# Transposes in blocks, queries and keys in one product, and a reordered opening in a two-layer encoder trunk

## The chip, the cores and the metric

The kernel runs on one core of a Trainium2 chip. The metric is device time in microseconds (us) of the one launch; lower is better. The kernel before takes 2476.66 us, the median of 3 runs (2476.47 to 2478.3).

## What is computed

A float32 input x of 256 tokens by 2048 features goes through two layers. Each layer is a normalised mixer with a residual, then a normalised gated feed-forward part with a residual, and a final RMSNorm follows. The reference, cut to its frame:

```python
for layer in range(DEPTH):                      # DEPTH = 2
    y = rmsnorm(h, ln_mix[layer])
    if layer % 2 == 0:                          # A: 8 heads x 3 dilated groups; B: 4 differential heads
        mix = even_mixer(y, ev_w_in[e], ev_w_out[e], ..., t5_table, lambda_init)
    else:                                       # C: 8 grouped-query heads with rotary; D: 8 neighbourhood heads
        mix = odd_mixer(y, od_w_in[o], od_w_out[o], gqa_q_norm[o], gqa_k_norm[o], na_rpb[o], rows)
    h = h + mix
    f = conv_ffn(rmsnorm(h, ln_ffn[layer]), ffn_w_up[layer], ffn_conv_w[layer], ffn_conv_b[layer], ffn_w_down[layer])
    h = h + f
return rmsnorm(h, ln_final)
```

The weights are float32 and are read once: 459 MB in all, for only 256 tokens.

## The kernel before

**Products in two parts.** Each float32 operand is split into a high and a low part, so that three fast products (high by high, high by low, low by high) give nearly full precision. ScalarE writes the high part (`S.copy`, L214), VectorE the low part (L217). A piece of a weight matrix, a *unit*, is 128 x 1024 numbers: `wunit` (L106) loads it on SP's queue into one of 5 buffers `raw` and splits it into `wh` and `wl`, of which there are 4 each.

**Two kinds of product.** `gemm_a` (V, output and down projections) takes the activations as the stationary operand and has 512 output columns; a unit has 12 matmuls of 512 columns (L178 to L180). The other kind takes a weight tile as the stationary operand and has [high | low] activations of 256 tokens as the moving one. It consists of H, a matmul with `wh` of 512 columns (`b_high`, L126), and L, a matmul with `wl` of 256 columns (`b_low`, L132). An output tile of 128 features needs 2 units, 16 H and 16 L. `gemm_b` makes one tile in the order 8 H, 8 L, 8 L, 8 H. `gemm_b2`, used in the feed-forward part, makes two tiles: 32 H, then 32 L.

**The order of the work.** Program order is written by hand. A small planner holds attention work back: `later(delay, fn, rank)` puts a piece into a list, and every `tick()` in the products moves a counter on by one and emits what is due, values (rank 0) before transposes (rank 1) before logits and softmax (rank 2). A query tile and a key tile are two calls of `gemm_b` (in `qk_tile`), each with its own tick; the attention on them has a delay of 2. A scheduler then goes through the program in that order and issues, on each engine, the first instruction that its own model takes to be ready; so instructions can move past each other within an engine, unless `tc.keep_in_program_order` pins one behind its predecessor on that engine.

**Transposes.** The residual `h` is turned into feature-major tiles `yT` by TensorE transposes into PSUM (`transposes`, L260). Two buffers `tp`, of one bank each, take four transposes each; two of them make one `yT` tile, which ScalarE and VectorE then read out and split (`y_tile`). In the program two transposes are followed by the reading of their half of the bank, and then by the next two. `to_features` (L735) and `b_finish` (L636) do the same. Softmax maps are transposed four at a time (`transposed_probs`, L363).

**The opening.** Eight steps `u` each load two tiles of x and a unit for two V products (`v_ps`), and between them: the rows of x (`x_rows`), their squares for the norm (`squares`), the loads (`rel_loads`, on SP) and the making (`rel_tables`) of a table of position biases, which takes two matmuls with a onehot matrix (L430, L431), an add (L433) and stores on GpSimd's queue. `row_factor` and `row_broadcast` make the norm's factor per token.

Of the kernel before, what the change touches and what calls it, by code (L numbers as in the profile page):

```python
# [58 lines left out]
def trunk_kernel(ctx: ExitStack, tc, a, out):  # L59
# [61 lines left out]
    def two(ap):  # L121
        return ap.rearrange("p (a b) -> p a b", a=2)
# [11 lines left out]

    def gemm_b(src, act):

        ps = two(tps("gm", 4))
        wh, wl = wunit(src[0])
        b_high(ps, wh, 0, act)
        b_low(ps, wl, 0, act)  # L140
        wh, wl = wunit(src[1])
        b_low(ps, wl, 1, act)
        b_high(ps, wh, 1, act)
        tick()
        return ps

    def gemm_b2(srcs, act, middle=lambda: None):

        pss = [two(tps("gm", 4)) for _ in srcs]
        low = []  # L150
        for u in range(2):
            for ps, src in zip(pss, srcs):
                wh, wl = wunit(src[u])
                b_high(ps, wh, u, act, last=False)
                low.append((ps, wl, u))
            if u == 0:
                middle()
# [5 lines left out]
        tick()  # L163
        return pss
# [75 lines left out]

    def squares(c, ts=(0, 1)):
        if c == 0:
            ssq_now[0] = tmp.tile([P, 2, 4], F32, name=nm("ssq"), tag="ssq")
        for t in ts:
            junk = tmp.tile([P, 512], F32, name=nm("junk"), tag="junk", bufs=1)
            S.activation(junk, hchunk(t, c), AF.Square, accum_out=ssq_now[0][:, t, c:c + 1])

    def y_tile(src, gain, kt, pin=False):
        y = acts.tile([P, 2, SEQ], F32R, name=nm("yT"), tag="yT", bufs=KT)
        split_scaled(y[:, 0, :], y[:, 1, :], src, gain[:, kt:kt + 1], pin)  # L250
        return y

    def transposes(c, gain, res):

        for b in range(2):
            ps = two(tps("tp", 2))
            for j in range(2):
                kt = c * 4 + b * 2 + j
                for t in range(2):
                    T.transpose(ps[:, j, t * P:(t + 1) * P], h[:, t, kt * P:(kt + 1) * P], ident)  # L260
                res.append(y_tile(ps[:, j, :], gain, kt))

    def row_factor():
        ss = tmp.tile([P, 2], F32, name=nm("ss"), tag="ss")
        V.tensor_reduce(ss, ssq_now[0], axis=AX.X, op=ALU.add)
        return rsqrt_mean(ss, D, "rstd", const)

    def row_broadcast(rstd, by_parity=False):

        ps = tps("tp", 2)  # L270
        for t in range(2):
            b = tmp.tile([P, P], F32, name=nm("rb"), tag="rb")
            V.tensor_copy(b, rstd[:, t:t + 1].to_broadcast([P, P]))
            T.transpose(ps[:, t * P:(t + 1) * P], b, ident)
# [43 lines left out]

    def qk_tile(src, act, r, order, slot):
        t = halves(gemm_b(src, act), r, order)  # L320
        y = new_qk("qk", slot)
        split(y[:, 0, :], y[:, 1, :], t)
        return y

# [33 lines left out]
    def transposed_probs(p0, p1, order=None):  # L358

        ps = two(tps("tp", 2))  # L360
        for kt in range(2):
            for t, p in enumerate((p0, p1)):
                T.transpose(ps[:, kt, t * P:(t + 1) * P], p[:, kt * P:(kt + 1) * P], ident)  # L363
        pt = new_pt()
        split(pt[:, :, 0, :], pt[:, :, 1, :], order(ps) if order else ps)
        return pt
# [54 lines left out]

    def rel_tables():

        table, onehot, bmask, bmask2 = rel_in
# [5 lines left out]
        T.matmul(ps[0:28, :], th, oh, start=True, stop=False)  # L430
        T.matmul(ps[0:28, :], tl, oh, start=False, stop=True)  # L431
        vals = tmp.tile([28, NREL + 1], F32, name="vals", tag="rw", bufs=1)
        V.tensor_tensor(vals, ps[0:28, :], bmask, op=ALU.add)  # L433
        G.dma_start(rel, vals)
        vals2 = tmp.tile([28, 256], F32, name="vals2", tag="t0")
        V.tensor_tensor(vals2, ps[0:28, :].rearrange("p (j r) -> p r j", r=2)[:, 1, :], bmask2, op=ALU.add)
        G.dma_start(rel2, vals2)

    rstd_par = const.tile([P, 2], F32, name="rstd_par")

    def parity_factor(R):

        ps = two(tps("tp", 2))
        for t in range(2):
            T.transpose(ps[:, t, 0:P], R[:, t * P:(t + 1) * P], ident)
        V.tensor_copy(rstd_par, ps[:, :, 0])

    v_ps = [[tps("gm", 4), tps("gm", 4)] for _ in range(2)]
    for u in range(8):
        xt = att.tile([P, 2, SEQ], F32, name=nm("xT"), tag=f"qk{2 + u % 4}", bufs=1)  # L450
        nc.sync.dma_start(xt.rearrange("p a b -> p (a b)"), a["xT"][u])
        x_tile(xt, u, 0)
        if u:
            x_tile(xt, u, 1)
        for g in range(2):
            a_unit(v_ps[g], a["eva_v"][g], u, yT, KT, parts=1 if u else 2,
                   between=None if u or g else lambda: x_tile(xt, 0, 1))
# [12 lines left out]
        tick()  # L470
# [72 lines left out]
    def a_head(hd, vg):  # L543
        sc = []
        for g in range(3):
            b = a_bias(hd, g)
            q = qk_tile(a["eva_qk"][hd * 6 + 2 * g], yT, Rq, rev, 2 * g)
            k = qk_tile(a["eva_qk"][hd * 6 + 2 * g + 1], yT, R, None, 2 * g + 1)
            if g == 0:
                later(2, lambda q=q, k=k, b=b: a_local(q, k, b, sc))  # L550
            else:
                later(2, lambda g=g, q=q, k=k, b=b: a_strided(g, q, k, b, sc))

        def soft():
            softmax(sc[0])
            later(2, lambda: a_transposes(sc[0], hd, vg), 1)
        later(2, soft)

    for hh in range(2):
        vg = []  # L560
        for g in range(3):
            ps = v_ps.pop(0) if v_ps else gemm_a(a["eva_v"][hh * 3 + g], yT, KT)
            if hh and g == 0:
# [68 lines left out]
    def b_finish(hd, o):  # L632
        ps = two(tps("tp", 2))
        for f in range(2):
            for t in range(2):
                T.transpose(ps[:, f, t * P:(t + 1) * P], o[:, t, f * P:(f + 1) * P], ident)  # L636
            y = new_act("mix", 8 + 2 * hd + f)
# [3 lines left out]
    for pair in range(2):  # L641
        vt = v_tiles(gemm_a(a["evb_v"][pair], yT, KT), rstd_par, range(20 - 4 * pair, 24 - 4 * pair))
        for hd in (2 * pair, 2 * pair + 1):
            bias = row_bias(24 + hd)
            sc = []
            for m in range(2):
                q = qk_tile(a["evb_qk"][hd * 4 + m], yT, Rq, rev, 2 * m)
                k = qk_tile(a["evb_qk"][hd * 4 + 2 + m], yT, R, None, 2 * m + 1)
                later(2, lambda m=m, q=q, k=k, sc=sc, bias=bias: b_logits(m, q, k, sc, bias))
# [4 lines left out]
    def ffn(layer, yT, gain, last=False):  # L654
        R = None
        res = None
        for half in range(2):
            prod = []
            for i in range(HALF_F):
                f = half * HALF_F + i  # L660
                srcs = [a["up"][layer, f, x] for x in range(2)]
                if f == 0:
# [4 lines left out]

                    pg, pu = gemm_b2(srcs, yT, first_units)
                else:
                    pg, pu = gemm_b2(srcs, yT)  # L670
                g = halves(pg, R)
# [57 lines left out]
    def to_features(ys, nh, slot):  # L729
        res = []  # L730
        for i in range(nh):
            if i % 2 == 0:
                ps = two(tps("tp", 2))
            for t in range(2):
                T.transpose(ps[:, i % 2, t * P:(t + 1) * P], ys[t][:, i, :], ident)  # L735
            q = new_qk("cq", slot + i)
            split(q[:, 0, :], q[:, 1, :], ps[:, i % 2, :])
            res.append(q)
        return res
# [52 lines left out]
    for hh in range(2):  # L792
        vt = v_tiles(gemm_a(a["od_v"][hh], yT, KT), rstd, ((18, 19, 20, 21), (16, 17, 22, 23))[hh])
        for hd in range(hh * 4, hh * 4 + 4):
# [6 lines left out]
            G.tensor_tensor(y, y, colmask.unsqueeze(1).to_broadcast([P, 6, 64]), op=ALU.add)  # L801
            q = qk_tile(a["od_qk"][hd * 2], yT, Rq, rev, hd % 2 * 2)
            k = qk_tile(a["od_qk"][hd * 2 + 1], yT, R, None, hd % 2 * 2 + 1)
            later(2, lambda hd=hd, q=q, k=k, vt=vt, y=y: d_head(hd, q, k, vt, y))
# [181 lines left out]
```

## Time and profile before

| | |
|---|---|
| median of 3 runs | 2476.66 us (2476.47 to 2478.3) |
| profiled execution | 2478.31 us, span 2476.5 us |
| TensorE matmuls | busy 2465.1 us (100%), 13113 of them |
| TensorE weight loads | busy 2124.5 us (86%) |
| VectorE, ScalarE | busy 1624.0 us (66%), 1252.4 us (51%) |
| GpSimd | busy 43.9 us (2%) |
| moved by DMA | 463.60 MB, mean 187 GB/s |

A profile is one execution. In the rows of the timeline the first number is the start in us from the start of the span, the second the time covered; then come engine, line, operation, output<-input and the count, and in brackets the idle time before and what ended it. Matmuls are pipelined, so that the durations of neighbours overlap: what one costs is read from start to start.

### The profile page before, as it was taken

The numbers are of one execution on the slowest core, as the hardware profiler recorded it, in microseconds if no ns is written. First come the engines' busy times: TensorE is split into PE (matmuls) and PEld (weight loads), VectorE is DVE, ScalarE is ACT, GpSimd is POOL, SyncE is SP. The second block draws the span as 40 slices with busy tenths as digits, with TensorE's granted clock in tenths as the row PEclk, the third lists the DMA queues.
The fourth block names the chain that finished last, engine by engine and source line by source line (L and its number), as shares of the span: only waits on it lengthen the run. The fifth ranks groups of instructions, "written<-read, shape, count | busy, mean of one in ns | idle before, by whom it ended". The sixth has DMA issues, their size and how long they took to land.

```text
span 2476.5 us, 34420 instructions
## 1 busy us (share of the span) xinstructions
PE 2465.1 (100%) x13113; PEld 2124.5 (86%) x13113; DVE 1624.0 (66%) x2462; ACT 1252.4 (51%) x1862; POOL 43.9 (2%) x71
## 2 busy tenths in 40 slices
PE   9999999999999999999999999999999999999998
PEld 7888888888888888888888888888888888888887
DVE  6676567676576775467775568665677655676754
ACT  6455455465555453445444457545554533545443
POOL 0000000000000000000000000100000000000000
PEclk9999999999999999999999999999999999999999
DMA  8655566556555556656556555765565566555564
GB/s 296 188 175 178 186 180 184 176 177 181 173 178 185 197 181 207 192 176 199 183 198 193 187 186 164 174 177 179 172 200 182 194 199 194 185 186 189 194 198 144
DMA packets 130282, 463.60 MB, mean 187 GB/s; under 512 B 15248, under 2 KB 15788, under 8 KB 130116
## 3 DMA queue, kind: packets, MB, share of 16 engines
q1 hardware_dynamic: 127124, 455.03, 56.2%
q0 software_dynamic: 2560, 6.08, 2.7%
q8 instruction: 102, 1.67, 0.3%
q14 instruction: 64, 0.52, 0.1%
q10 hardware_dynamic: 432, 0.30, 0.0%
HBM read 459.16 MB, written 2.18 MB: 186 GB/s over the span
## 4 chain that ended last, share of the span: by engine, by line
PE 100%; DVE 0%; ACT 0%; issue 0%; DVEq 0%
PE gm L126 38%; PE gm L132 20%; PE gm L179 13%; PE gm L180 13%; PE gm L178 13%; PE tp L363 0%; PE tp L260 0%; PE s L340 0%; PE s L339 0%; PE s L341 0%; PE s L534 0%; PE s L503 0%; PE s L401 0%; PE s L375 0%; PE s L527 0%; PE s L374 0%
## 5 line engine op out<-in xcount | busy, mean ns | idle before, releaser
L217 DVE TENSOR_TENSOR wl<-raw,wh 128x1024 fp32r<-128x1024 f32 (+1 forms) x858 | 1039.0, 1221 | 557.6 <-ACT wh L214 389.8
L214 ACT CAST wh<-raw 128x1024 fp32r<-128x1024 f32 (+1 forms) x858 | 899.7, 1049 | 735.9 <-PE gm L180 419.4
L126 PE MATMUL gm<-yT,wh 128*128 128x512 f32 x4096 | 974.1, 391 | 0.0
L126 PEld LDWEIGHTS gm<-yT,wh 128*128 128x128 f32 x4096 | 754.5, 188 | 148.4 <-DVE yT L223 0.7
L132 PEld LDWEIGHTS gm<-yT,wl 128*128 128x128 f32 x4096 | 513.5, 191 | 13.3
L132 PE MATMUL gm<-yT,wl 128*128 128x256 f32 x4096 | 517.6, 283 | 0.0
L207 ACT COPY t<-gm 128x256 f32<-128x256 f32 x256 | 95.4, 373 | 360.3 <-PE gm L132 203.6
L178 PE MATMUL gm<-wh,prod 128*128 128x512 f32 x704 | 274.6, 390 | 0.0
L180 PE MATMUL gm<-wh,prod 128*128 128x512 f32 x704 | 274.2, 390 | 0.0
L179 PE MATMUL gm<-wl,prod 128*128 128x512 f32 x704 | 274.0, 389 | 0.0
L208 DVE TENSOR_TENSOR t<-t,gm 128x256 f32<-128x256 f32 x256 | 106.4, 416 | 101.2 <-ACT t L207 101.2
L179 PE MATMUL gm<-wl,yT 128*128 128x512 f32 x416 | 163.6, 393 | 1.6 <-DVE wl L217 1.6
L178 PE MATMUL gm<-wh,yT 128*128 128x512 f32 x416 | 163.4, 395 | 0.0
L180 PE MATMUL gm<-wh,yT 128*128 128x512 f32 x416 | 163.4, 393 | 0.0
L179 PEld LDWEIGHTS gm<-wl,prod 128*128 128x128 f32 x704 | 132.2, 188 | 27.3
L178 PEld LDWEIGHTS gm<-wh,prod 128*128 128x128 f32 x704 | 132.2, 188 | 27.2
L180 PEld LDWEIGHTS gm<-wh,prod 128*128 128x128 f32 x704 | 132.1, 188 | 27.2
L178 PE MATMUL gm<-wh,mix 128*128 128x512 f32 x256 | 101.1, 395 | 0.0
L179 PE MATMUL gm<-wl,mix 128*128 128x512 f32 x256 | 100.4, 392 | 0.0
L180 PE MATMUL gm<-wh,mix 128*128 128x512 f32 x256 | 100.3, 393 | 0.0
L179 PEld LDWEIGHTS gm<-wl,yT 128*128 128x128 f32 x416 | 79.1, 190 | 17.6 <-DVE wl L217 2.0
L180 PEld LDWEIGHTS gm<-wh,yT 128*128 128x128 f32 x416 | 78.7, 189 | 16.7
(216 smaller groups left out, 1496.4 us busy)
## 6 DMA issues: line engine op xcount, KB each, us to landing
raw<-in_up SPq DMA_DIRECT2D x352, 512.0 KB, 4.3
raw<-in_down SPq DMA_DIRECT2D x176, 512.0 KB, 4.3
raw<-in_eva_qk SPq DMA_DIRECT2D x96, 512.0 KB, 3.5
raw<-in_eva_v SPq DMA_DIRECT2D x46, 512.0 KB, 4.1
raw<-in_evb_qk SPq DMA_DIRECT2D x32, 512.0 KB, 3.4
raw<-in_ev_out SPq DMA_DIRECT2D x32, 512.0 KB, 3.5
raw<-in_od_qk SPq DMA_DIRECT2D x32, 512.0 KB, 3.8
raw<-in_od_out SPq DMA_DIRECT2D x32, 512.0 KB, 3.3
```

Source lines behind the costliest of these rows:

```text
L126: T.matmul(ps.rearrange("p a b -> p (a b)"), wh[:, k * P:(k + 1) * P], act[u * 8 + k].rearrange("p a b -> p (a b)"), start=(u == 0 and k = ...
L132: T.matmul(ps[:, 1, :], wl[:, k * P:(k + 1) * P], act[u * 8 + k][:, 0, :], start=False, stop=(last and u * 8 + k == KT - 1))
L178: T.matmul(ps[t], ah, wh[:, sl], start=(kt == 0), stop=False)
L179: T.matmul(ps[t], ah, wl[:, sl], start=False, stop=False)
L180: T.matmul(ps[t], al, wh[:, sl], start=False, stop=(kt == nk - 1))
L207: S.copy(t0, ps[:, 0, :])
L208: V.tensor_tensor(t0, t0, ps[:, 1, :], op=ALU.add)
L214: first = S.copy(dst_h, src)
L217: V.tensor_tensor(dst_l, src, dst_h.bitcast(F32), op=ALU.subtract)
```

## The change

It does four things. **(a)** In the opening, the squares, the row factor, the transposes of the row factor, the two matmuls of the table and its add are pinned in program order; the rows of x are loaded earlier, the table later, its product and its add are parted (units 5 and 7), and the first V product is read out inside unit 7. **(b)** `transpose_block` emits all transposes of a chunk, a head or a set of features one after the other, each pinned behind the one before; the reading comes after them. Chunks of h now take both `tp` banks at once. **(c)** `gemm_b2` takes the name and place of `gemm_b`; queries and keys are made by one call, `qk_tiles`. **(d)** Its two ticks become one `tick(2)`, placed between the 32 H and the 32 L, so that everything that is due in a pair is emitted there together.

```diff
-    def tick():
-        now[0] += 1
+    def tick(n=1):
+        now[0] += n
         due = sorted((p for p in pending if p[0] <= now[0]), key=lambda p: p[1])
...
-    def gemm_b2(srcs, act, middle=lambda: None):
+    def gemm_b(srcs, act, middle=lambda: None):
         pss = [two(tps("gm", 4)) for _ in srcs]
         low = []
         for u in range(2):
             for ps, src in zip(pss, srcs):
                 wh, wl = wunit(src[u])
                 b_high(ps, wh, u, act, last=False)
                 low.append((ps, wl, u))
             if u == 0:
                 middle()
+        tick(2)
         for ps in pss:
             for x in low:
                 if x[0] is ps:
                     b_low(*x, act, last=True)
-        tick()
-        tick()
         return pss
...
+    def transpose_block(pairs):
+        for i, (dst, src) in enumerate(pairs):
+            ins = T.transpose(dst, src, ident)
+            if i:
+                tc.keep_in_program_order(ins)
...
     def transposes(c, gain, res):
-        for b in range(2):
-            ps = two(tps("tp", 2))
-            for j in range(2):
-                kt = c * 4 + b * 2 + j
-                for t in range(2):
-                    T.transpose(ps[:, j, t * P:(t + 1) * P], h[:, t, kt * P:(kt + 1) * P], ident)
-                res.append(y_tile(ps[:, j, :], gain, kt))
+        ps = [two(tps("tp", 2)) for _ in range(2)]
+        transpose_block([(ps[j // 2][:, j % 2, t * P:(t + 1) * P], h[:, t, (c * 4 + j) * P:(c * 4 + j + 1) * P])
+                         for j in range(4) for t in range(2)])
+        for j in range(4):
+            res.append(y_tile(ps[j // 2][:, j % 2, :], gain, c * 4 + j))
...
+    def qk_tiles(srcs, act, rs, orders, slot):
+        res = []
+        for x, ps in enumerate(gemm_b(srcs, act)):
+            t = halves(ps, rs[x], orders[x])
+            y = new_qk("qk", slot + x)
+            split(y[:, 0, :], y[:, 1, :], t)
+            res.append(y)
+        return res
...
             if u == 6 and g == 0:
-                R = row_broadcast(row_factor(), by_parity=True)
+                R = row_broadcast(row_factor(pin=True), by_parity=True)
             if u == 6 and g == 1:
                 parity_factor(R)
-        if 2 <= u < 6:
-            squares(u - 2)
-        if 1 <= u < 5:
-            x_rows(u - 1)
-        if u == 3:
+            if u == 7 and g == 0:
+                v_first = v_tiles(v_ps[0], rstd_par, range(8, 12))
+        for c in {3: (0,), 4: (1, 2), 5: (3,)}.get(u, ()):
+            squares(c, pin=True)
+        for c in {1: (0,), 2: (1,), 3: (2, 3)}.get(u, ()):
+            x_rows(c)
+        if u == 4:
             rel_loads()
         if u == 5:
-            rel_tables()
+            rel_ps = rel_products()
+        if u == 7:
+            rel_tables(rel_ps)
```

`rel_products` holds the two matmuls of the old `rel_tables` (the first one pinned), the new `rel_tables` the two adds (the first one pinned) and the stores. `transposed_probs`, `b_finish` and `to_features` call `transpose_block`, the last with all its features in one block. The heads of A, B and D call `qk_tiles` with the two weight tiles that they gave to `qk_tile` one by one.

More of the change, by code (lines that the diff above doesn't have):

```diff
@@ L239, in hchunk, with squares @@
         return h[:, t, c * 512:(c + 1) * 512]
-    def squares(c, ts=(0, 1)):
+    def squares(c, pin=False):
         if c == 0:
             ssq_now[0] = tmp.tile([P, 2, 4], F32, name=nm("ssq"), tag="ssq")
-        for t in ts:
+        for t in range(2):
             junk = tmp.tile([P, 512], F32, name=nm("junk"), tag="junk", bufs=1)
-            S.activation(junk, hchunk(t, c), AF.Square, accum_out=ssq_now[0][:, t, c:c + 1])
+            ins = S.activation(junk, hchunk(t, c), AF.Square, accum_out=ssq_now[0][:, t, c:c + 1])
+            if pin:
+                tc.keep_in_program_order(ins)
     def y_tile(src, gain, kt, pin=False):
@@ L251, in y_tile, with row_factor @@
         return y
[L253 to L263 removed]
+    def transpose_block(pairs):
+        for i, (dst, src) in enumerate(pairs):
+            ins = T.transpose(dst, src, ident)
+            if i:
+                tc.keep_in_program_order(ins)
+    def transposes(c, gain, res):
+        ps = [two(tps("tp", 2)) for _ in range(2)]
[3 more added lines that the diff above has]
+            res.append(y_tile(ps[j // 2][:, j % 2, :], gain, c * 4 + j))
+    def row_factor(pin=False):
         ss = tmp.tile([P, 2], F32, name=nm("ss"), tag="ss")
[L265 removed]
+        ins = V.tensor_reduce(ss, ssq_now[0], axis=AX.X, op=ALU.add)
+        if pin:
+            tc.keep_in_program_order(ins)
         return rsqrt_mean(ss, D, "rstd", const)
@@ L273, in row_broadcast @@
             V.tensor_copy(b, rstd[:, t:t + 1].to_broadcast([P, P]))
-            T.transpose(ps[:, t * P:(t + 1) * P], b, ident)
+            ins = T.transpose(ps[:, t * P:(t + 1) * P], b, ident)
+            if by_parity:
+                tc.keep_in_program_order(ins)
         r = const.tile([P, SEQ], F32, name=nm("R"), tag="R", bufs=1)
@@ L317, in new_qk @@
         return att.tile([P, 2, SEQ], F32R, name=nm(name), tag=f"qk{slot}", bufs=1)
[L319 to L323, printed above, removed]
+    def qk_tiles(srcs, act, rs, orders, slot):
[6 more added lines that the diff above has]
+        return res
     def v_tiles(ps, rstd, slots):
@@ L360, in transposed_probs @@
         ps = two(tps("tp", 2))
-        for kt in range(2):
-            for t, p in enumerate((p0, p1)):
-                T.transpose(ps[:, kt, t * P:(t + 1) * P], p[:, kt * P:(kt + 1) * P], ident)
+        transpose_block([(ps[:, kt, t * P:(t + 1) * P], p[:, kt * P:(kt + 1) * P])
+                         for kt in range(2) for t, p in enumerate((p0, p1))])
         pt = new_pt()
@@ L420, in rel_loads, with rel_products @@
             rel_in.append(load(name, (28 if "bmask" in name else 32, width), pool=tmp, tag=tag, eng=nc.sync))
-    def rel_tables():
-        table, onehot, bmask, bmask2 = rel_in
+    def rel_products():
+        table, onehot = rel_in[:2]
         th, tl = (tmp.tile([32, 28], F32R, name=nm("t5"), tag=f"t5{x}", bufs=1) for x in range(2))
@@ L429, in rel_tables @@
         ps = tps("s", 2)
-        T.matmul(ps[0:28, :], th, oh, start=True, stop=False)
+        tc.keep_in_program_order(T.matmul(ps[0:28, :], th, oh, start=True, stop=False))
         T.matmul(ps[0:28, :], tl, oh, start=False, stop=True)
+        return ps
+    def rel_tables(ps):
+        bmask, bmask2 = rel_in[2:]
         vals = tmp.tile([28, NREL + 1], F32, name="vals", tag="rw", bufs=1)
-        V.tensor_tensor(vals, ps[0:28, :], bmask, op=ALU.add)
+        tc.keep_in_program_order(V.tensor_tensor(vals, ps[0:28, :], bmask, op=ALU.add))
         G.dma_start(rel, vals)
@@ L444, in parity_factor @@
         for t in range(2):
-            T.transpose(ps[:, t, 0:P], R[:, t * P:(t + 1) * P], ident)
+            tc.keep_in_program_order(T.transpose(ps[:, t, 0:P], R[:, t * P:(t + 1) * P], ident))
         V.tensor_copy(rstd_par, ps[:, :, 0])
@@ L546, in a_head @@
             b = a_bias(hd, g)
-            q = qk_tile(a["eva_qk"][hd * 6 + 2 * g], yT, Rq, rev, 2 * g)
-            k = qk_tile(a["eva_qk"][hd * 6 + 2 * g + 1], yT, R, None, 2 * g + 1)
+            q, k = qk_tiles([a["eva_qk"][hd * 6 + 2 * g + x] for x in range(2)], yT, (Rq, R), (rev, None), 2 * g)
             if g == 0:
@@ L561, in trunk_kernel @@
         for g in range(3):
-            ps = v_ps.pop(0) if v_ps else gemm_a(a["eva_v"][hh * 3 + g], yT, KT)
+            if not hh and g == 0:
+                vg.append(v_first)
+                continue
+            ps = v_ps[1] if not hh and g == 1 else gemm_a(a["eva_v"][hh * 3 + g], yT, KT)
             if hh and g == 0:
@@ L633, in b_finish @@
         ps = two(tps("tp", 2))
+        transpose_block([(ps[:, f, t * P:(t + 1) * P], o[:, t, f * P:(f + 1) * P])
+                         for f in range(2) for t in range(2)])
         for f in range(2):
-            for t in range(2):
-                T.transpose(ps[:, f, t * P:(t + 1) * P], o[:, t, f * P:(f + 1) * P], ident)
             y = new_act("mix", 8 + 2 * hd + f)
@@ L646, in trunk_kernel @@
             for m in range(2):
-                q = qk_tile(a["evb_qk"][hd * 4 + m], yT, Rq, rev, 2 * m)
-                k = qk_tile(a["evb_qk"][hd * 4 + 2 + m], yT, R, None, 2 * m + 1)
+                q, k = qk_tiles([a["evb_qk"][hd * 4 + 2 * x + m] for x in range(2)], yT, (Rq, R), (rev, None), 2 * m)
                 later(2, lambda m=m, q=q, k=k, sc=sc, bias=bias: b_logits(m, q, k, sc, bias))
@@ L730, in to_features @@
         res = []
+        ps = [two(tps("tp", 2)) for _ in range(nh // 2)]
+        transpose_block([(ps[i // 2][:, i % 2, t * P:(t + 1) * P], ys[t][:, i, :])
+                         for i in range(nh) for t in range(2)])
         for i in range(nh):
[L732 to L735, printed above, removed]
             q = new_qk("cq", slot + i)
-            split(q[:, 0, :], q[:, 1, :], ps[:, i % 2, :])
+            split(q[:, 0, :], q[:, 1, :], ps[i // 2][:, i % 2, :])
             res.append(q)
@@ L801, in trunk_kernel @@
             G.tensor_tensor(y, y, colmask.unsqueeze(1).to_broadcast([P, 6, 64]), op=ALU.add)
-            q = qk_tile(a["od_qk"][hd * 2], yT, Rq, rev, hd % 2 * 2)
-            k = qk_tile(a["od_qk"][hd * 2 + 1], yT, R, None, hd % 2 * 2 + 1)
+            q, k = qk_tiles([a["od_qk"][hd * 2 + x] for x in range(2)], yT, (Rq, R), (rev, None), hd % 2 * 2)
             later(2, lambda hd=hd, q=q, k=k, vt=vt, y=y: d_head(hd, q, k, vt, y))
```

14 lines of the change are left out of this document (2 added, 12 removed).

## The prediction

> **What bounds the kernel now.** I read the page first: span, busy shares and the chain that ended last.
>
> ```profile
> span 2476.5 us, 34420 instructions
> PE 2465.1 (100%) x13113; PEld 2124.5 (86%) x13113; DVE 1624.0 (66%) x2462; ACT 1252.4 (51%) x1862; POOL 43.9 (2%) x71
> PE 100%; DVE 0%; ACT 0%; issue 0%; DVEq 0%
> PE gm L126 38%; PE gm L132 20%; PE gm L179 13%; PE gm L180 13%; PE gm L178 13%; PE tp L363 0%; PE tp L260 0%; PE s L340 0%; PE s L339 0%; PE s L341 0%; PE s L534 0%; PE s L503 0%; PE s L401 0%; PE s L375 0%; PE s L527 0%; PE s L374 0%
> ```
>
> The chain is TensorE from end to end. The change adds and removes no matmul, so only two things can move the time: idle time or lost clock on TensorE, and what it costs to go from one kind of matmul to another. The waits of that engine come next; this is the only one on another engine's work after the opening matmuls of zeros.
>
> ```profile
> PE gm L179 <- DVE wl L217: 1.6, 1, 1.6
> ```
>
> **The price of one matmul.** The timeline of TensorE, in an attention stage and then in the feed-forward part (start, duration, line, tile, count):
>
> ```profile
> 103.20 3.82 PE L126 MATMUL gm<-yT,wh 128*128 128x512 f32 x16
> 106.85 2.08 PE L132 MATMUL gm<-yT,wl 128*128 128x256 f32 x16
> 108.76 2.00 PE L126 MATMUL gm<-yT,wh 128*128 128x512 f32 x8
> 110.61 0.28 PE L503 MATMUL s<-qk,qk 128*128 128x256 f32 x1
> ...
> 111.01 2.08 PE L126 MATMUL gm<-yT,wh 128*128 128x512 f32 x8
> 112.93 2.07 PE L132 MATMUL gm<-yT,wl 128*128 128x256 f32 x16
> ...
> 692.08 4.00 PE L132 MATMUL gm<-yT,wl 128*128 128x256 f32 x32
> 695.92 1.32 PE L126 MATMUL gm<-yT,wh 128*128 128x512 f32 x5
> ```
>
> From start to start, 16 H (L126) take 106.85 - 103.20 = 3.65 us, 228 ns each (I use 227, since the rows are rounded to 0.01 us; with 228 each excess worked out below would be 0.02 to 0.04 smaller); 16 L (L132) take 108.76 - 106.85 = 1.91 us, 119 ns each. The feed-forward part already runs in the order that queries and keys are to get, and there 32 L take 695.92 - 692.08 = 3.84 us, 120 ns each. So **the order H, L inside a product costs nothing either way**: the regrouping itself is priced at zero, and what hides nothing needs no cover. From 108.76 to 112.93 stand 16 H (3.63) and four logits (two of 256 columns at 0.12, two of 128 at 0.06, 0.36): 3.99 of 4.17 us, so such an insertion loses some 0.15 us, by its 128-column matmuls.
>
> **Part 1, the pins in the opening.** TensorE first, then VectorE and ScalarE, then the stage as a whole (length, PE busy and count, granted clock, DMA share, GB/s):
>
> ```profile
> 28.24 0.41 PE L430 MATMUL s<-onehot_r,t 32*28 32x512 f32 x1
> 28.49 0.39 PE L431 MATMUL s<-onehot_r,t 32*28 32x512 f32 x1
> 28.81 0.73 PE L178 MATMUL gm<-wh,yT 128*128 128x512 f32 x2
> 31.12 0.79 PE L179 MATMUL gm<-wl,yT 128*128 128x512 f32 x1 [1.58 <-DVE wl L217]
> 31.70 0.63 PE L180 MATMUL gm<-wh,yT 128*128 128x512 f32 x1
> ...
> 34.64 0.40 PE L179 MATMUL gm<-wl,yT 128*128 128x512 f32 x1
> ```
> ```profile
> 28.92 0.68 DVE L433 TENSOR_TENSOR vals<-s,bmask 28x512 f32<-28x512 f32 x1 [3.38 <-PE s L431]
> 29.86 2.34 DVE L217 TENSOR_TENSOR wl<-raw,wh 128x1024 fp32r<-128x1024 f32 x2
> ```
> ```profile
> 24.93 2.07 ACT L214 CAST wh<-raw 128x1024 fp32r<-128x1024 f32 x2
> 28.51 0.63 ACT L246 ACTIVATE junk<-h 128x512 f32<-128x512 f32 x1 [1.51 <-DMA h<-in_x]
> 29.05 0.19 ACT L246 ACTIVATION_READ_ACCUMULATOR junk<-h 128x1 f32 x1
> ```
> ```profile
> 27.92:34.64 6.72, 5.14 (x14) 0.75 0.91 337
> ```
>
> The bias table's add (L433) stands in VectorE's queue ahead of two low parts wl and waits 3.38 us for the onehot product on TensorE. The high parts of the same unit were done at 27.00. So wl is late, TensorE stands still for 1.58 us, and then its clock is halved: matmuls of 0.63 us at steps of 0.43 from 31.70 to 34.26. Between 27.92 and 34.64 thirteen matmuls start, which at 227 ns are 2.95 us; 3.77 us are lost. About 0.32 us of that belongs to the onehot pair itself (its own steps are 0.25 and 0.32 us, and the ones beside it are as long) and stays. The change pins the pair behind unit 5, and the add behind unit 7, where the product is some 11 us old: **3.45 us come free**, of which 1.74 are the stall and 1.7 the slow clock.
>
> What is moved past what: on SP the four table loads go behind the weights of unit 4, and the rows of x come earlier (two chunks at unit 3). The weights of unit 4 then wait for one more chunk (0.5 MB; at the 337 GB/s of the window above 1.6 us) but for no table. On ScalarE the squares of two chunks are pinned behind unit 4's casts: four of 0.63 + 0.19 us, 3.3 us. By my count of units (24 matmuls, 5.45 us each) unit 4's last cast ends near 24.6, the squares near 27.9, unit 5's wl near 31.1, and TensorE asks for it at 33.6: 2.5 us to spare. GpSimd's stores of the two tables come some 20 us later; their first readers are the logits of the first pair, behind the third V product (192 matmuls, 44 us). Bounds: nothing gained if this margin is used up and a like stall forms one unit later, 1.7 us lost beyond that if it costs a second slow stretch; 3.77 at best. I take 3.45.
>
> TensorE's page in the Trainium skill ("TensorE: Matmul & The Clock Gate", Part 1, The HAM clock gate) says that the clock is halved after an idle window of about 3.4 us, in a free-running grid. By that rule a pause of 1.58 us would not cost the clock, and part 1 would be worth 1.74 us, the sum 2473.0; here the slow stretch after it is in the rows, and the trace decides. The free-running grid would explain why some runs may pay for it and others not.
>
> **Part 2, transposes in blocks.** Stages with the transposes of h (L260) scattered, and one of to_features (L735), in the same columns:
>
> ```profile
> 640.86:651.57 10.71, 10.71 (x56) 1.00 0.50 158
> 685.77:692.08 6.31, 6.31 (x32) 1.00 0.22 81
> 1327.73:1333.12 5.39, 5.39 (x29) 1.00 0.60 197
> 1477.10:1480.84 3.74, 3.74 (x22) 1.00 0.86 281
> ```
>
> and a place where eight already stand in one block:
>
> ```profile
> 171.57 0.60 PE L363 MATMUL tp<-ident,sc 128*128 128x128 f32 x4
> 172.00 0.60 PE L516 MATMUL tp<-ident,sc 128*128 128x128 f32 x4
> 172.36 0.36 PE L339 MATMUL s<-qk,qk 128*128 128x256 f32 x1
> 172.56 0.28 PE L340 MATMUL s<-qk,qk 128*128 128x256 f32 x1
> ```
>
> In the block, eight cost 172.56 - 171.57 = 0.99 less the logit's 0.12: 0.87 us, 109 ns each with both edges. Scattered, the first stage has 16 transposes (1.74) and 38 matmuls (8.63; the count in the row has two more still running at its edge): 0.34 us over, for two chunks. The second has 8, two more of the row factor (1.09) and 21 matmuls (4.77): 0.45 over. The third has 8 (0.87) and 19 (4.31): 0.21 over. The excess comes where two write half of a bank while the other half is still being read. A mixer's end is then 0.34 + 0.2 + 0.45, twice, and the feed-forward end four times 0.21: 2.8 us for twelve chunks. To_features has 0.14 over in the row shown (8 and 12 matmuls), perhaps 0.4 in all, and b_finish like the T pairs perhaps 0.3. In blocks I keep 0.02 each and 0.03 for the row factors: **3.1 us come free**. The block needs two free tp banks and delays the first matmul behind it by up to 0.87 us, but that is order, not work. Bounds: 0 (the bank waits move to the blocks' starts) and 3.5 (all of the excess).
>
> **Part 3, queries and keys together.** The 40 pairs keep their 64 matmuls. Attention that was inserted at every tile now goes in once a pair, so values and strided logits stand side by side and lose one return to long matmuls: of the 0.15 us lost at such a place perhaps a third, eight times, and less for the other heads. I take **0.5 us**, between 0 and 2.4 (0.15 at 16 strided places). The price can also be below nothing. The logits are issued behind 32 H, 7.3 us after their keys' last matmul; before it was 64 matmuls, 11.1 us. How long the chain of a key takes:
>
> ```profile
> 122.44 0.37 ACT L207 COPY t<-gm 128x256 f32<-128x256 f32 x1 [2.66 <-PE gm L126]
> ```
> ```profile
> 126.45 0.41 DVE L217 TENSOR_TENSOR qk<-t,qk 128x256 fp32r<-128x256 f32 x1
> ```
>
> And the attention stage by engine (PE, PEld, DVE, ACT, POOL):
>
> ```profile
> 100.00:247.00 147.00, 147.00 (x851) 129.33 (x850) 102.55 (x162) 75.65 (x119) 6.43 (x12) 1.00 0.60 178
> ```
>
> Copy to last split, 126.86 - 122.44 = 4.4 us, with a softmax and two weight splits in between: 2.9 us of cover are left. Behind a late logit on TensorE stand the 32 L, the next pair's H and everything after; without cover each 0.1 us late costs 4 us over 40 pairs.
>
> **The sum.** 3.45 + 3.1 + 0.5 = 7.05 us. The profiled execution took 2478.31 us, 1.8 beyond its span; less 7.05 this is **2471.3 us**. It is the slowest of the runs shown (2476.47, 2476.66, 2478.3), and 1.65 above their median, which is one slow stretch of clock (1.7): I take it that the median run had the stall without it, gains only 5.35 and comes to the same 2471.3, 0.22% below 2476.66. A measurement of this kernel can tell about 0.2% (5 us) from no change, so the forecast lies at that edge.
>
> **Rivals.**
> - *The clock is not what parts the runs.* Then all 7.05 come off the median: 2469.6. For it: I see the clock of one run only. Against: the fit of 1.65 to 1.7.
> - *The opening's wait moves*: the pinned squares make unit 5's high part late and part 1 gives nothing, 2471.3 + 3.45 = 2474.7. For it: ScalarE gets 6.3 us of work in a unit of 5.45. Against: 2.5 us of margin.
> - *The blocks give nothing*, since the first of each waits for its banks: 2471.3 + 3.1 = 2474.4. For it: the two banks are now taken at once. Against: the chunk before is a whole product of 16 us older.
> - *Slower: the logits come late.* Place: the middle of each pair, TensorE waiting for the key's split. It decides from a chain of 7.3 us against 4.4 measured. If it is late by 0.3 us in all 40 pairs, 12 us are lost: 2483.3. For it: halves of both tiles, four weight splits and softmax now fall together in VectorE's queue, which is 102.55 of 147 us busy in this stage, 70%. Against: the feed-forward part runs the same order with no TensorE wait.
> - *Slower by the clock.* Eight transposes in a row are taken for idleness and twelve blocks each bring a slow stretch of 1.7 us: 2471.3 + 20.4 = 2491.7. The clock around the block of eight shown above:
>
> ```profile
> 170.00:175.00 5.00, 5.00 (x31) 1.00 0.66 198
> ```
>
> It stayed full, so I give it almost nothing. This is the rule of the same page, Part 4 (PE-mode transpose), that transposes do not count as busy for the clock gate; the rows bear it out in no place.
>
> **How the numbers follow.** Forecast 0.58, with a range of its own of 2469.4 to 2472.9 (part 3 at its 2.4, or half of part 2 lost); clock rival 0.10; opening 0.12; blocks 0.06; late logits 0.12; clock by transposes 0.02. Faster by over 0.2% means under 2471.7: some six tenths of the forecast (0.36) and the clock rival, 0.46. Within 0.2%: the rest of the forecast (0.22) and the two rivals near 2474.5, 0.40. Slower: 0.14. The range reaches from 2468.8, where part 3 gives 1.3 us instead of 0.5 and the clock rival holds, to 2477.0, where the opening and most of part 2 fail together.
>
> **What would show it.** Part 1: no TensorE wait on wl near 30 us, and a clock of 1.00 from 7 us on. Part 2: the transposes of h in runs of eight, and stages like those above at 0.87 us per block. Part 3: 32 H, attention, 32 L with steps of 227 and 120 ns. Wrong would be any TensorE wait on a split of qk, on a bank of tp, or on wl after the opening; or a total that falls by more than these excesses hold.

## The result and the profile after

The changed kernel takes 2484.83 us, median of 8 runs (2483.77 to 2485.69), against 2476.44 for the kernel before (8 runs, 2476.25 to 2478.3): a ratio of 1.0032, 95% interval 1.0023 to 1.004. It is slower by 8.4 us; 2471.3 was forecast. The profiled execution took 2484.88 us.

The page of the kernel after: span, busy shares and the chain that ended last.

```profile
span 2483.1 us, 34345 instructions
PE 2464.7 (99%) x13113; PEld 2130.5 (86%) x13113; DVE 1611.9 (65%) x2462; ACT 1258.5 (51%) x1862; POOL 42.6 (2%) x71
PE 96%; DMA 2%; DVE 1%; ACT 1%; issue 0%; SPq 0%; DVEq 0%; ACTq 0%
```

The busy times are hardly different, and the count of matmuls is the same. But the chain is no longer TensorE from end to end: 4% of it are other engines and loads. The waits of TensorE (line, what it waited for, us in total, times, longest):

```profile
PE s L344 <- DVE mix L207: 4.0, 1, 4.0
PE s L344 <- ACT qk L204: 2.4, 1, 2.4
PE s L405 <- DVE zeros L402: 1.5, 1, 1.5
PE gm L169 <- DVE wl L207: 1.3, 2, 1.0
PE s L345 <- DVE qk L207: 0.5, 1, 0.5
```

Before there was one wait of 1.6 us on `wl`, besides the matmuls of zeros at the start. Now there are waits of logits (L344, L345) on the split of a key (`qk`) and on that of a head output (`mix`). Each stands once: they belong to three places, not to all pairs. TensorE in the first two of them:

```profile
569.44 7.45 PE L126 MATMUL gm<-yT,wh 128*128 128x512 f32 x32
576.72 0.60 PE L248 MATMUL tp<-ident,sc 128*128 128x128 f32 x4
579.77 0.38 PE L344 MATMUL s<-qk,qk 128*128 128x256 f32 x1 [2.45 <-ACT qk L204]
580.22 0.38 PE L345 MATMUL s<-qk,qk 128*128 128x256 f32 x1
...
581.26 5.16 PE L132 MATMUL gm<-yT,wl 128*128 128x256 f32 x32
586.26 0.40 PE L168 MATMUL gm<-wh,mix 128*128 128x512 f32 x1
...
1568.19 0.58 PE L344 MATMUL s<-qk,qk 128*128 128x256 f32 x1 [3.98 <-DVE mix L207]
...
1569.64 5.45 PE L132 MATMUL gm<-yT,wl 128*128 128x256 f32 x29
1574.93 0.40 PE L168 MATMUL gm<-wh,yT 128*128 128x512 f32 x1
```

This is the new order, 32 H, attention, 32 L, and TensorE stands still in its middle. After the pause the 32 L take 586.26 - 581.26 = 5.00 us instead of 3.84; at the second place 29 of them take 5.29 instead of 3.48. The three places as windows (length, TensorE busy and count, granted clock, DMA share, GB/s):

```profile
576.72:586.26 9.54, 7.02 (x44) 0.82 0.28 98
1561.83:1574.93 13.10, 9.12 (x56) 0.74 0.56 125
1643.04:1651.19 8.15, 6.70 (x52) 1.00 0.41 133
```

With 0.12 us for a matmul of 256 columns, 0.11 for a transpose and 0.227 for one of 512 columns, the first window holds 5.00 us of work (4 transposes, 6 logits, 32 L), the second 6.4 (18 matmuls of attention, 4 transposes, 32 L), the third 6.2 (12, 4, 32 L and the first two matmuls of the next product). **4.5, 6.7 and 2.0 us are lost there, 13.2 in all.** About 4.2 of that is lower clock: 0.18 x 9.54 = 1.7 in the first window; in the second, where part of the low clock falls into the pause itself, 2.5 by the steps behind the pause (6 logits take 1.45 us instead of 0.72, the 29 L 5.29 instead of 3.48). All three are the last pair of a stage: the next weights are those of an output or value projection.

Who is late? ScalarE at the first place, then at the second:

```profile
571.95 1.05 ACT L204 CAST wh<-raw 128x1024 fp32r<-128x1024 f32 x1
577.09 1.04 ACT L204 CAST wh<-raw 128x1024 fp32r<-128x1024 f32 x1 [4.09 <-DMA raw<-in_ev_out]
578.36 1.04 ACT L204 CAST wh<-raw 128x1024 fp32r<-128x1024 f32 x1 [0.23 <-DMA raw<-in_ev_out]
579.31 0.40 ACT L204 CAST qk<-t 128x256 fp32r<-128x256 f32 x1
...
1563.67 1.04 ACT L204 CAST wh<-raw 128x1024 fp32r<-128x1024 f32 x1 [4.30 <-DMA raw<-in_od_v]
...
1567.32 0.64 ACT L204 CAST mix<-s 128x256 fp32r<-128x256 f32 x2
```

The key `t` was ready at 575.53, since VectorE wrote it then:

```profile
575.11 0.42 DVE L200 TENSOR_TENSOR t<-t,R 128x256 f32<-128x256 f32 x1
579.75 0.42 DVE L207 TENSOR_TENSOR qk<-t,qk 128x256 fp32r<-128x256 f32 x1 [4.21 <-ACT qk L204]
```

At the first place the key's cast stands on ScalarE behind two casts of the *next* stage's weights, and ScalarE waits 4.09 us for a load. At the second place the queue stands 4.30 us for a load, and the two head outputs behind it keep the two PSUM banks `s` that the logits want. The third place is mixed. One logit waits 0.5 us for VectorE, which does a weight split ahead of the key's split; no load is in this. The projection behind the pair waits 1.0 us for its low part: VectorE has stood 2.99 us at a head output, whose cast stands on ScalarE behind one that waits 1.70 us for its load. That load took no longer than others, 3.3 us, but went out only at 1643.15.

Why is the load late at the first two places? The bandwidth in 40 slices of 0.75 us from 555 us on, and the issues of the stretch (KB each, median us from issue to landing):

```profile
GB/s 0 0 0 218 355 169 82 388 235 131 355 290 317 208 49 0 0 49 44 41 41 33 22 68 227 363 401 399 421 426 328 180 33 16 0 0 0 0 0 0
raw<-in_ev_out SPq DMA_DIRECT2D x6, 512.0 KB, 7.7
```

Hardly anything is moved from 565.5 to 573; then the loads run together at up to 426 GB/s and land together, 7.7 us after their issue. Two things meet here. SP can issue the four loads only from 568.94 on, since their buffers come free only as the held low parts are used. And GpSimd's queue has sent a table of the next stage (`nb`, two loads of 96 KB) 2 us ahead of them, at 566.78. The rows of both queues, and the DMA engines' share by queue from 568.5 to 572.5 (packets, MB, share of the 16 engines; q0 is GpSimd's, and SP's q1 has no row in this stretch):

```profile
566.78 1.32 POOL L811 DMA_DIRECT2D nb<-in_rpb  x2 [40.61 <-DVE sc L602]
568.94 4.60 SPq L111 DMA_DIRECT2D raw<-in_ev_out  x4
q0 software_dynamic: 60, 0.14, 101.5%
```

For those 4 us the table's load takes all 16 engines and moves 0.14 MB, and the weights, though issued, move nothing. The table goes out when VectorE's add (L602) has read the buffer that it is written to, and that add belongs to the attention which the change has put into the middle of a pair. At the second place it is the same: the table at 1554.38, four loads from 1555.28 on that take 5.6 to 8.3 us. SP's queue does not wait longer in all: its waits at L111 sum to 2124 us before and 2120 after. Its loads only go out at other times.

That gives a theory with four steps. **Q, the queue:** (1) in the paired order all four low parts `wl` are held until the 32 L; (2) so the next units' low parts can't be written, their `raw` buffers stay taken, and SP's loads stop, then go out together, at the first two places behind the table, and land late; (3) the scheduler's order has put the casts that depend on these loads ahead of the key's or the head output's cast; (4) ScalarE, which works its queue in order, stands at the load, and TensorE behind it. Its rivals: **B, the banks**: the inserted block wants three `s` banks and has two. **C, the cover**: a chain of 4.4 us or more simply doesn't fit under 32 H.

### The profile page after: what moved, and what is told of

It is laid out like the page before. It is cut to its first block, busy times and chain, and to the rows that moved or that the text cites. A ratio compares the mean times of both kernels' runs of the same rounds, so it can differ in the third digit from the quotient of the medians.

```text
span 2483.1 us, 34345 instructions
## 1 busy us (share of the span) xinstructions
PE 2464.7 (99%) x13113; PEld 2130.5 (86%) x13113; DVE 1611.9 (65%) x2462; ACT 1258.5 (51%) x1862; POOL 42.6 (2%) x71
## 4 chain that ended last, share of the span: by engine, by line
PE 96%; DMA 2%; DVE 1%; ACT 1%; issue 0%; SPq 0%; DVEq 0%; ACTq 0%
PE gm L126 36%; PE gm L132 19%; PE gm L169 12%; PE gm L170 12%; PE gm L168 12%; PE tp L248 1%; DMA raw<-in_eva_v 1%; DVE wl L207 0%; DMA xT<-in_xT 0%; PE s L344 0%; PE s L345 0%; ACT wh L204 0%; DMA raw<-in_ev_out 0%; PE s L346 0%; DMA raw<-in_od_v 0%
## 5 line engine op out<-in xcount | busy, mean ns | idle before, releaser
L126 PE MATMUL gm<-yT,wh 128*128 128x512 f32 x4096 | 954.6, 390 | 0.1
```

The lines of the kernel that those rows point to most:

```text
L126: T.matmul(ps.rearrange("p a b -> p (a b)"), wh[:, k * P:(k + 1) * P], act[u * 8 + k].rearrange("p a b -> p (a b)"), start=(u == 0 and k = ...
```

## The experiments

**Which part costs it: `p12`, `p3`.** `p12` takes the pairs out again and keeps the pins and the blocks; `p3` puts only the pairs into the kernel before.

```diff
 p12, against the kernel after:
-        for x, ps in enumerate(gemm_b(srcs, act)):
-            t = halves(ps, rs[x], orders[x])
+    def qk_tile(src, act, r, order, slot):
+        t = halves(gemm_b(src, act), r, order)      # gemm_b: 8 H, 8 L, 8 L, 8 H, tick() after each tile
```

> The changed kernel with part 3 undone: queries and keys are two products of one tile each again (8 H, 8 L, 8 L, 8 H, a tick after each), pins and blocks stay. In the changed kernel TensorE lost 4.5, 6.7 and 2.0 us at three places in the pairs (near 577, 1562 and 1643 to 1651 us of its span). If the pairs cause these, they vanish here: 2484.8 - 13.2 + 0.5 (the merged attention work) = 2472. If the blocks of transposes or the pins in the opening cause them, they stay and the time is 2480 or more.

> The kernel before with part 3 alone: pairs of 32 H, due work, 32 L; no pins, no blocks. If the pairs alone bring the three waits: 2476.4 + 13.2 - 0.5 = 2489. If it takes the blocks or the opening as well, fewer waits and less than 2482.

`p12` took 2473.59 us (2472.92 to 2473.88), ratio 0.9985 [0.9977, 0.9994] to the 2476.89 of the kernel before on that chip. `p3` took 2487.47 (2485.5 to 2489.24), 1.0041 [1.0028, 1.0055]. TensorE's waits in `p12`, then in `p3`:

```profile
PE s L411 <- DVE zeros L408: 1.5, 1, 1.5
PE gm L179 <- DVE wl L217: 0.5, 1, 0.5
```
```profile
PE s L333 <- DVE mix L207: 3.7, 1, 3.7
PE gm L169 <- DVE wl L207: 2.7, 3, 1.6
PE s L333 <- ACT qk L204: 2.4, 1, 2.4
```

The pairs alone carry the whole loss: +10.6 us put onto the kernel before, +11.2 (2484.83 - 2473.59; 11.7 if each is taken against its own kernel before) put onto the other two parts. With them come the same waits in the same places, without them none. In `p12` the same four loads go out from 561.9 to 569.5, ahead of the table at 572.59, and land in 3.3 to 4.6 us.

**Past the queue: `dvecast`.** The high parts of queries, keys and of the head outputs of the second layer are written by VectorE, so that ScalarE's queue can't hold them up. The loads stay as they are.

```diff
+    def split_v(dst_h, dst_l, src):
+        V.tensor_copy(dst_h, src)
+        V.tensor_tensor(dst_l, src, dst_h.bitcast(F32), op=ALU.subtract)
...
-            split(y[:, 0, :], y[:, 1, :], t)
+            split_v(y[:, 0, :], y[:, 1, :], t)
...
-        split(o[:, 0, :], o[:, 1, :], ps)
+        split_v(o[:, 0, :], o[:, 1, :], ps)
```

> The changed kernel, but the high parts of q and k, and of the head outputs of C and D, are written by VectorE in place of ScalarE, so that they no longer stand in ScalarE's queue behind weight casts that wait for a DMA. Theory Q (queue: late loads hold up ScalarE, and with it what the logits need): most of 13.2 us comes back, 2472 to 2474. Theory B (bank: three s banks are wanted in one block of attention work and there are two): the place near 577, which has no such shortage, is cured, the others stay, 2480. Theory C (cover: 32 H are too short for the chain of a key): no change or slower, 2484 to 2487.

2476.24 us (2475.28 to 2476.69), 0.9994 [0.9986, 1.0003]: no difference from the kernel before, and 8.6 of the 11.2 us are back. Its ScalarE and its TensorE at the first place:

```profile
577.08 1.05 ACT L204 CAST wh<-raw 128x1024 fp32r<-128x1024 f32 x1 [4.42 <-DMA raw<-in_ev_out]
...
577.03 0.36 PE L348 MATMUL s<-qk,qk 128*128 128x256 f32 x1
...
583.35 0.50 PE L169 MATMUL gm<-wl,mix 128*128 128x512 f32 x1 [1.30 <-DVE wl L207]
```

ScalarE still stands 4.42 us at the same load, but the logits start right behind the transposes, at 577.03 instead of 579.77. The loads are as late as ever (7.5 to 8.1 us). What is left is their lateness itself, now at the first matmul that needs a low part, and 0.8 us at a logit of the third place, which waits for VectorE. The late load and the queue are two things, and the queue was the dear one.

**Shorter cover without held low parts: `inter_a`.** Queries and keys are still made together, but as 16 H, 16 L, attention, 16 H, 16 L. That leaves a key only 16 H and 16 L (5.6 us) of cover, less than the 7.3 of the change, but gives two low parts free in the middle.

```diff
+        for u in range(2):
+            low = []
+            for ps, src in zip(pss, srcs):
+                wh, wl = wunit(src[u])
+                b_high(ps, wh, u, act, last=False)
+                low.append((ps, wl, u))
+            for x in low:
+                b_low(*x, act, last=True)
+            if u == 0:
+                tick(2)
```

> The changed kernel, but a pair runs 16 H, 16 L, due attention work, 16 H, 16 L, so that low weight parts come free twice as early and loads start earlier; attention comes 16 H and 16 L (5.6 us) behind the pair before, sooner than the 7.3 us of the changed kernel. Q: no late loads, no waits, 2471 to 2473. C: less cover, more waits, over 2490. B: the same work stands in one block, two of the three places stay, 2480.

2474.64 us (2473.45 to 2475.24), 0.999 [0.9981, 0.9998]. No weight cast of queries or keys waits for its load any more; at the first place three loads go out from 563.2 to 567.4, ahead of the table at 568.24, and land in 3.2 to 4.6 us. One logit does wait, and again it is a queue that stands at a load, this time VectorE's, at a small table:

```profile
413.09 0.42 DVE L606 TENSOR_TENSOR lprod<-lvec 128x256 f32<-128x256 f32 x1 [4.33 <-DMA lvec<-in_lvec]
...
418.69 0.39 PE L360 MATMUL s<-qk,qk 128*128 128x256 f32 x1 [0.98 <-DVE qk L222]
```

With less cover nearly all of the loss is gone: C falls as a cause by itself.

**More cover, low parts still held: `latetick`.** The due attention goes behind the 32 L: one line moved, 11.1 us of cover.

```diff
-        tick(2)
         for ps in pss:
             for x in low:
                 if x[0] is ps:
                     b_low(*x, act, last=True)
+        tick(2)
```

> The changed kernel with the due attention work behind the 32 L in place of ahead of them: logits come 64 matmuls (11.1 us) behind their key, loads and queues stay as they are. In the changed kernel the key's high part near 577 is ready 8 us after the key's last matmul. If the wait is this lateness against 7.3 us of cover: gone, and the places near 1562 and 1643 too, 2473 to 2475. Theory B (three s banks in one block): the same work still stands in one block, two of three places stay, 2480.

2472.35 us (2471.96 to 2473.03), 0.9981 [0.9973, 0.999]. One moved line does two things here: there is more cover, and the table, whose buffer that attention frees, goes out at 571.69, behind three of the loads. The low parts are held as before and the loads still come close together, the three from 568.26 to 570.86, but they now land in 3.1 to 4.8 us, and no cast at these places waits for one:

```profile
571.69 1.33 POOL L811 DMA_DIRECT2D nb<-in_rpb  x2 [44.57 <-DVE sc L602]
raw<-in_ev_out SPq DMA_DIRECT2D x3, 512.0 KB, 4.7
```

Of TensorE's waits in the pairs only this is left, and it is the most that B can be worth by itself:

```profile
PE s L344 <- DVE mix L207: 0.3, 1, 0.3
```

**One more load buffer: `raw6`.** Six `raw` instead of five. The place comes from two tables of the second layer that go into idle buffers of activations, and from another scratch for the squares' unused output.

```diff
-RAW = 5
+RAW = 6
...
-    cossin = load("cossin", (P, 2, 2, 64))
+    cossin = load("cossin", (P, 2, 2, 64), pool=acts, tag="act22")
```

> The changed kernel with six load buffers in place of five (room made by laying two small constant tables into idle activation buffers, and the squares' waste output into another scratch buffer). One more load is in flight while the low weight parts are held. Theory Q: ScalarE's casts find one more load landed, the waits near 577, 1562 and 1643 get shorter or vanish, 2473 to 2480. Theories B and C: no change, 2484 to 2486.

2476.77 us (2476.24 to 2478.75), 1.0 [0.9991, 1.0009]. The same places are smaller:

```profile
PE s L344 <- DVE mix L207: 2.4, 2, 1.6
PE s L344 <- ACT qk L204: 1.5, 1, 1.5
```

4.0 became 2.4 in two waits and 2.4 became 1.5; 8 us came back with no product moved. The sixth buffer lets one more load go out ahead of the table. The three behind it still take 7.9 to 8.4 us. So buffers decide when a load goes out, and the table ahead of it decides how long it takes: at the first place, behind the table 7.5 to 8.4 us in the kernel after, `dvecast` and `raw6`; ahead of it 3.1 to 4.8 in `p12`, `inter_a` and `latetick`. This is read from the traces; no run moves the table alone.

**The other two parts alone: `p1`, `p2`.** `p1` is the kernel before with the pinned opening, `p2` with the blocks.

```diff
 p1 (of the opening's edits):
+        for c in {3: (0,), 4: (1, 2), 5: (3,)}.get(u, ()):
+            squares(c, pin=True)
 p2:
+        transpose_block([(ps[j // 2][:, j % 2, t * P:(t + 1) * P], ...) for j in range(4) for t in range(2)])
```

> The kernel before with part 1 alone (the pins and the new order of the opening). The prediction gave this part 3.45 us in an execution whose clock slows after the stall, 1.75 in one whose clock does not. In the profile of parts 1 and 2 together the opening still loses 1.1 us near 33, which was not foreseen: 3.8 - 1.1 - 0.3 = 2.4 us with the slow clock, 0.7 without. Expected 2476.2; if the prediction's size holds, 2475.1.

> The kernel before with part 2 alone (transposes in blocks). The prediction gave this part 3.1 us; from the steps of TensorE in the profile of parts 1 and 2 it is 1.7: 2475.2. If the prediction's size holds, 2473.8.

`p1` took 2475.62 (2475.07 to 2476.2), 0.9993 [0.9984, 1.0002], 1.05 us under the 2476.67 of the kernel before, with an interval that includes no change; `p2` 2474.42 (2473.88 to 2476.12), 0.999 [0.9981, 0.9998], 2.25 under it. Together that is 3.3, which is what `p12` shows (2476.89 - 2473.59). The opening in `p1` is not clean: as in the kernel after, a wait has moved one unit on. ScalarE and TensorE of the kernel after:

```profile
31.39 0.18 ACT L236 ACTIVATION_READ_ACCUMULATOR junk<-h 128x1 f32 x1
31.48 0.89 ACT L210 ACTIVATE yT<-xT,ln 128x256 fp32r<-128x256 f32 x2
32.28 1.99 ACT L204 CAST wh<-raw 128x1024 fp32r<-128x1024 f32 x2
...
33.71 0.61 PE L168 MATMUL gm<-wh,yT 128*128 128x512 f32 x2
34.63 0.50 PE L169 MATMUL gm<-wl,yT 128*128 128x512 f32 x1 [0.30 <-DVE wl L207]
```

Four squares and the onehot cast fill ScalarE to 31.57, unit 5's high parts end at 34.27, and its `wl` is asked for 0.45 us after 33.71, at 34.16. The profile of `p2` has the opening of the kernel before, and answers the question of its clock:

```profile
27.66:32.80 5.14, 3.56 (x14) 2.03 (x13) 4.10 (x8) 4.08 (x9) 1.20 (x2) 1.00 0.97 355
```

The same 14 matmuls take 5.14 us at a clock of 1.00, where the kernel before had 6.72 at 0.75: the stall is there, the slow stretch behind it is not.

**A version that beats both: `late_sq`, `p12_sq`, `late_min`, `inter_b_sq`.** `late_sq` is `latetick` with one square per unit in the opening; `p12_sq` is `p12` with the same squares, so that the two differ by the pairs alone. `late_min` is `latetick` with the squares, the rows of x and the table's loads where the kernel before has them, and only the product, the add and the row factor pinned, the last with its transposes. `inter_b_sq` has those squares and the order 16 H, 16 L, 16 H, attention, 16 L (9.2 us of cover, two low parts held).

```diff
 late_sq:
-        for c in {3: (0,), 4: (1, 2), 5: (3,)}.get(u, ()):
+        for c in {2: (0,), 3: (1,), 4: (2,), 5: (3,)}.get(u, ()):
 inter_b_sq, between the 16 H and the 16 L of the second unit:
+            if u == 1:
+                tick(2)
```

> The kernel with the due attention work behind the 32 L, and in the opening the squares of one chunk per unit (units 2 to 5, still pinned) in place of two chunks at unit 4. In its parent the opening loses 1.4 us near 33, where ScalarE has the squares of three chunks between two units' casts. If the squares make unit 5's casts late, about 1.2 us come back: 2471.2. If the loads do (ScalarE waited 5.4 us for them), no change: 2472.4.

> Parts 1 and 2 without pairs, with the squares of one chunk per unit. If the squares cost the 1.1 us near 33: 2472.5. Against late_sq it shows what the pairs are worth where they cause no wait: the prediction says 0.5 us, so late_sq 0.5 below this one.

> The same, but squares, rows of x and table loads in the places and without the pins that they had in the kernel before; only the table's product and add and the row factor stay pinned, and the first V product is read out early. If the pin of the add alone ends the opening's stall: 2471.0, as good as or better than the other. If the order of loads is needed too, the opening loses 1 us or more: 2472 to 2474.

> A pair runs 16 H, 16 L, 16 H, due attention work, 16 L (logits 9.2 us behind their key), with the squares of one chunk per unit. Q: loads early and cover above the 8 us that the slowest key took: no waits in the pairs, 2471.2.

The kernel before took 2477.43 on the same chip:

| | us | ratio, interval |
|---|---|---|
| `late_sq` | 2471.39 (2471.0 to 2471.9) | 0.9974 [0.9965, 0.9984] |
| `late_min` | 2471.38 (2470.93 to 2471.64) | 0.9976 [0.9966, 0.9986] |
| `inter_b_sq` | 2471.47 (2471.05 to 2471.65) | 0.9975 [0.9965, 0.9985] |
| `p12_sq` | 2472.76 (2472.38 to 2473.09) | 0.9981 [0.9972, 0.999] |

TensorE's waits in `late_sq`:

```profile
...
PE s L344 <- DVE mix L207: 0.3, 1, 0.3
```

Both orders of the pairs (`late_sq` and `late_min` share one) come to the same time, some 6 us under the kernel before and 13.4 under the change. With attention behind the 32 L, the pairs are worth 2472.76 - 2471.39 = 1.4 us. In `inter_b_sq` three loads at the first place went out ahead of the table, but the two behind it still took over 7 us; with that and 9.2 us of cover no logit waits. (The 8 us that two of the expectations give for the slowest key count from its copy at 571.68; from its last matmul it is 10 us.)

## Why the prediction was wrong

**The step that failed** is in part 3: "the regrouping itself is priced at zero, and what hides nothing needs no cover". The matmuls do cost the same: the order H, L is free on TensorE. But the order also says how long the four `wl` are held, and with that when `raw` comes free, when SP loads and when ScalarE can cast; and the place of attention says when the table on GpSimd's queue goes out. Part 3 was put down as a gain of 0.5 us (0 to 2.4, with the remark that the price could be below nothing) and came to a loss of 11.2. The prediction listed what the change moves on SP's queue for the opening, and left it out for the pairs, where at the first place the next stage's loads went out 2 us behind the table and took 7.6 to 8.1 us to land.

**The slower rival** had the place right, the middle of a pair, with TensorE waiting for a key's split. It had the size and the mechanism wrong. It reckoned with VectorE at 70% and with 0.3 us in each of 40 pairs; it is ScalarE standing at a load, which costs 4.5 and 6.7 us in two pairs and a part of 2.0 in a third; only there VectorE's own queue is late, by 0.5. Both sums are of one size (12 and 13.2) by chance. "The feed-forward part runs the same order with no TensorE wait" was no argument. The loads stop there too, for 2 to 4 us at a time, as the bandwidth of the kernel after from 750 to 780 us shows (40 slices of 0.75 us):

```profile
GB/s 350 268 322 295 366 197 153 360 175 22 0 0 0 71 224 404 322 350 344 300 126 262 339 55 0 0 0 0 82 311 317 208 273 393 404 208 224 382 27 0
```

But no table goes ahead of them: they land in a median of 4.2 us, little over the 3.5 of the projection's loads in `p12`, and no attention stands behind their casts.

```profile
raw<-in_up SPq DMA_DIRECT2D x10, 512.0 KB, 4.2
```

And 7.3 us of cover against a chain of 4.4 looked safe only because the 4.4 came from a stage in which no load was late.

**The balance of part 3.** 13.2 us lost in the three windows, less 1.4 gained in the other pairs (if they gain what `late_sq` shows), is 11.8, against 11.2 measured; the usual loss of an inserted block, 0.15 in each window, explains 0.45 of the rest.

**Part 1**: 3.45 us expected with the slow stretch, 1.74 without. `p1` gave 1.05 at the median, not clear of noise. The stall went as foretold, but the 2.5 us of margin for the pinned squares weren't there: the rival "the opening's wait moves" came true for about 1 us of it, which the other places of the squares give back (2472.35 to 2471.39 from `latetick` to `late_sq`, on two chips). As `late_min` shows, the pins of the squares and the moved loads aren't needed at all: its opening has no wait on `wl`, with the product and its add parted and pinned, the row factor pinned and the first V product read out early. Which of these is enough was not tested.

**The clock of the median run** was taken to be full. The window of `p2` shows the stall without the slow stretch, and the runs of the kernel before lie in two groups, near 2476.4 and near 2478.5, 2.1 us apart, near the 1.7 of that stretch. So the assumption is likely right, though no trace of the nearer group was taken of the kernel before itself. The rule of the Trainium skill weighed against the row ("TensorE: Matmul & The Clock Gate", Part 1, The HAM clock gate, idle window of about 3.4 us) would allow neither the slow stretch behind 1.58 us in the kernel before nor the one behind 2.45 us at 577. That the window is free-running, which the Trainium skill says in the same section, would fit a stall that costs the clock in one execution and not in another; no run here shows the window itself.

**Part 2**: 3.1 us expected, 2.25 measured (`p2`, median). The term that was too large is the chunks at a mixer's end and at the hand-over: there the block still waits for its banks and the row factor. By the steps of TensorE, the first mixer's end keeps 0.28 us of its 0.34 in `p2` and the hand-over behind it 0.35 of its 0.45; the six other chunks fall from about 0.21 to 0.03. Where the banks are free the sum is right; a run of eight in the kernel after costs the 0.87 taken, 0.79 us to the next start and 0.08 more in that matmul's own step of 0.31:

```profile
1326.86 1.03 PE L248 MATMUL tp<-ident,h 128*128 128x128 f32 x8
1327.65 0.48 PE L168 MATMUL gm<-wh,prod 128*128 128x512 f32 x1
1327.96 0.39 PE L169 MATMUL gm<-wl,prod 128*128 128x512 f32 x1
```

"Slower by the clock" from blocks of transposes is shown by no run: in the windows read here the clock fell only behind pauses.

## What to carry to other kernels

When an order of matmuls is changed, ask not only what TensorE pays, but which buffers are now held longer, which loads wait for them, what other queue's transfer now goes out ahead of them, and what stands in the in-order queue behind the instruction that needs such a load. A cheap cast that TensorE needs soon must not stand behind one that depends on a transfer, least of all at the end of a stage, where the next weights belong to another product. A wait of a few us that appears once in the list of waits can outweigh a saving repeated forty times.

## What the runs showed of the hardware

Pauses of TensorE of 2.45 and 3.98 us were each followed by a stretch of lower clock that cost 1.7 and 2.5 us; the 1.58 us pause of the opening cost 1.7 us in the profile of the kernel before and nothing in that of `p2`, which has the same opening. A table of 192 KB, loaded on GpSimd's queue, kept all 16 DMA engines for 4 us while it moved 0.14 MB of it. Loads of 512 KB issued behind that table took 7.6 to 8.1 us to land, and loads issued as close together but ahead of it (`latetick`) 3.1 to 4.8.
